# Rotary scores on one core: four of the 64 output stores issued as two transfers of 64 rows

## The chip, the cores and the metric

The kernel runs on one core of a Trainium2 chip. The metric is the device time of one execution in microseconds (us), shown as the median of several runs; one further execution is recorded by the hardware profiler, and all durations of single instructions and transfers come from that one.

## The reference

q and k have the shape (16, 512, 16, 64): 16 batches, 512 positions, 16 heads, 64 values, all float32. Both are rotated by position, and then each query is multiplied with each key of its batch and head:

```
q_rot = [q1*cos - q2*sin, q1*sin + q2*cos]      # q1, q2: the halves of the 64 values
k_rot = [k1*cos - k2*sin, k1*sin + k2*cos]
scores = einsum('bshd,bthd->bsht', q_rot, k_rot)   # (16, 512, 16, 512)
```

The inputs are 67 MB, the output is 268 MB. Nothing is reduced away: every score is written to HBM.

## The kernel before

**Tiling.** A batch is cut into four parts of 128 positions (C = 4); position 4p + c lies on partition p of part c. There are so 64 steps, numbered i = 4 * batch + part. One step makes one output tile `st` of 128 partitions (query positions) by 16 heads by 512 key positions, that is 128 rows of 32 KB, 4 MB in all. The same row of a tile lies in one piece in HBM; rows of neighbouring partitions are 128 KB apart there.

**Work of one step** (loop at line 264 for steps 4 to 63). VectorE rotates the q part of step i + 2 and the k part of step i + 5 (`rope`, lines 149 to 154). TensorE transposes rotated parts by 128x128 blocks (line 170), and VectorE or ScalarE copies the four blocks of a bank to SBUF (line 185). Eight times per step, for two heads each, TensorE multiplies (line 201) and ScalarE copies the 128x1024 result from PSUM into `st` (line 208). After the eighth copy, `store` (line 188) issues the whole tile as one DMA from the queue of SyncE (SP). In steps 0 to 3 the tile goes out in four pieces of 1 MB instead (line 211).

**Buffers.** `st` has three buffers. ScalarE's first copy of step i therefore waits until the store of step i - 3 has landed. The inputs of q and k have two buffers each.

**Order of the DMAs.** SP issues everything in the order of the program: a store per step, and behind the store of each step with i % 4 = 2 the load of a batch of q, behind that with i % 4 = 3 a load of a batch of k (2 MB each, line 122). Each issue uses one of eight completion semaphores in turn, and waits until the transfer that used it eight issues earlier has landed.

**Loads that go around one engine.** Five loads (`RELIEVED`, line 74: q of batch 6, k of 7, q of 11, k of 12, q of 15) are issued in pieces (`load_around`, line 86): rows 0 to 119 from GpSimd (POOL) at line 98, and rows 120 to 127 either from POOL (both k loads) or from SP (the q loads, line 111). Small transfers into `scratch` (line 84) before them set at which of the 16 DMA engines POOL's next transfer begins. The loads of q 11 and k 12 are issued around steps 38 and 39.

Of the kernel before, what the change touches and what calls it, by code (L numbers as in the profile page):

```python
# [10 lines left out]
def kernel(  # L11
# [8 lines left out]
    nc = tc.nc  # L20
# [6 lines left out]
    P = 128  # L27
    C = S // P
# [18 lines left out]
    o_v = out.rearrange("b (p c) h t -> b c p h t", c=C)  # L47
# [137 lines left out]
        copy(out=dst, in_=src)  # L185

    def store(i, st):
        nc.sync.dma_start(o_v[i // C, i % C], st)

    def scores(i, p, st):  # L190

        ps = ps_s_pool.tile([P, 2, S], fp32, tag="ps_s", name="ps")
        b = i // C
        if b == 0:
            c, hp = divmod(p, 2)
            lhs, rhs = qT[i][:, C * hp + c], kT[0][:, 2 * i + hp]
        else:
            lhs, rhs = qT[i][:, p], kT[b][:, p]
        for r in range(2):
            po, rh = ps[:, r, :], rhs[64 * r : 64 * r + 64, :]  # L200
            nc.tensor.matmul(  # L201
                out=po, lhsT=lhs[64 * r : 64 * r + 64, :], rhs=rh, start=True, stop=True
            )
        so, si = st[:, 2 * p : 2 * p + 2, :], ps
        if b > 0:
            so = so.rearrange("s r (t c) -> s r t c", c=C)
            si = si.rearrange("s r (c t) -> s r t c", c=C)
        nc.scalar.copy(out=so, in_=si)  # L208
        if b == 0 and p % 2 == 1:
            c = p // 2  # L210
            nc.sync.dma_start(o_v[0, c, :, G * i : G * (i + 1)], st[:, G * c : G * (c + 1)])
        elif b > 0 and p == HP - 1:
            store(i, st)
# [9 lines left out]
    with tc.manual_schedule():  # L223
# [15 lines left out]
        for i in range(C):  # L239
            st = st_first[i] if i < 2 else stage_pool.tile([P, H, S], fp32, tag="stage", name="st")  # L240
# [6 lines left out]
            for p in range(HP):  # L247
# [7 lines left out]
                if p in (2, 6):  # L255
                    m = len(dve) - (4 if p == 2 else 2) - (2 if i == C - 1 else 0)
# [7 lines left out]
        for i in range(C, NST):  # L264
# [10 lines left out]
            st = stage_pool.tile([P, H, S], fp32, tag="stage", name="st")  # L275
# [45 lines left out]
```

## Time and profile before

| | us |
|---|---|
| time, median of 3 runs (lowest to highest) | 793.13 (792.44 to 794.04) |
| span of the profiled execution, first to last instruction | 790.4 |
| TensorE busy (share of the span) | 684.4 (87%) |
| ScalarE busy | 562.0 (71%) |
| VectorE busy | 544.7 (69%) |
| GpSimd busy | 11.9 (2%) |
| from issue to landing of a 4 MB store, median | 24.7 |

The time of the profiled execution itself is not given apart from its span; the median lies 2.7 us above the span, which is what passes ahead of the first and behind the last instruction. The page gives busy time for each compute engine, the busy share and rate of the 16 DMA engines together, the chain of work that ended last, and groups of instructions with the idle time in front of them and what ended it. A "window" below is a stretch of the span in us from its start.

### The profile page before, as it was taken

Reading aid. Unit: us, or ns where it says so; the run is one execution under the profiler, and the core shown is the slowest. Engines: PE = TensorE matmul, PEld = TensorE weight load, DVE = VectorE, ACT = ScalarE, POOL = GpSimd, SP = SyncE. Lnnn points to the kernel's source line nnn. Section 1 sums busy time; section 2 is a strip of 40 time slices with the busy share of each in tenths; the row PEclk is TensorE's granted clock in tenths of the full one; section 3 lists DMA queues with packets and bytes.
Section 4 is the critical chain, followed back from the end, with each engine's and each line's share of the span. In section 5 each row is a group of like instructions: output and inputs, shape, how many; then the busy total and the mean of one; then the engine's idle time right before and its main releaser. Section 6 shows DMA issues by size and latency. Waiting matters only on the chain.

```text
span 790.4 us, 7750 instructions
## 1 busy us (share of the span) xinstructions
PE 684.4 (87%) x3072; PEld 296.4 (38%) x3072; DVE 544.7 (69%) x516; ACT 562.0 (71%) x647; POOL 11.9 (2%) x24
## 2 busy tenths in 40 slices
PE   4989998988988889798996989889899798799960
PEld 2444443433433334343342433334334343344420
DVE  6999988666766678576785767667678487587400
ACT  3888886865857768486785866777577586588770
POOL 0000000000001000000000001000000000000000
PEclk9999999998999999898998989999899899899995
DMA  9999999999999999999999999999999999999997
GB/s 357 417 425 439 429 430 435 425 435 436 429 429 428 413 432 419 433 423 438 433 427 436 426 432 429 422 432 424 430 432 427 436 429 432 430 432 434 432 429 340
DMA packets 18836, 336.18 MB, mean 425 GB/s; under 512 B 2312, under 2 KB 3592, under 8 KB 4616
## 3 DMA queue, kind: packets, MB, share of 16 engines
q1 hardware_dynamic: 16704, 325.46, 96.4%
q0 software_dynamic: 1808, 10.10, 3.1%
q8 instruction: 24, 0.39, 0.2%
q10 hardware_dynamic: 288, 0.13, 0.1%
q14 instruction: 12, 0.10, 0.0%
HBM read 67.24 MB, written 268.44 MB: 425 GB/s over the span
## 4 chain that ended last, share of the span: by engine, by line
DMA 49%; PE 40%; ACT 5%; DVE 3%; issue 1%; ACTq 0%; SPq 0%; DVEq 0%
DMA out_dram<-st 46%; PE ps L201 30%; PE bank L170 10%; ACT st L208 5%; DMA q_sb<-in_q_dram 2%; DVE part L149 1%; DMA early<-in_k_dram 1%; DVE q_sb L150 0%; DVE k_sb L154 0%; DVE k_sb L150 0%; DVE q_sb L154 0%; DVE early L150 0%; DVE kT_t L185 0%; ACTq L316 0%; DVE early L154 0%
## 5 line engine op out<-in xcount | busy, mean ns | idle before, releaser
L208 ACT COPY st<-ps 128x1024 f32<-128x1024 f32 x512 | 495.7, 1020 | 192.6 <-DMA out_dram<-st 109.8
L201 PE MATMUL ps<-kT_t,qT_t 64*128 64x512 f32 x2048 | 544.0, 649 | 67.0 <-ACT st L208 67.0
L201 PEld LDWEIGHTS ps<-kT_t,qT_t 64*128 64x128 f32 x2048 | 183.6, 196 | 256.2 <-issue 133.3
L185 DVE COPY qT_t<-bank 128x512 f32<-128x512 f32 x118 | 81.6, 691 | 193.9 <-PE bank L170 193.9
L170 PEld LDWEIGHTS bank<-ident,q_sb 128*128 128x128 f32 x480 | 54.2, 149 | 99.0 <-issue 96.4
L170 PEld LDWEIGHTS bank<-ident,k_sb 128*128 128x128 f32 x480 | 50.3, 140 | 96.4 <-DVE k_sb L150 39.5
L170 PE MATMUL bank<-ident,q_sb 128*128 128x128 f32 x480 | 85.1, 304 | 0.9 <-PE ps L201 0.9
L170 PE MATMUL bank<-ident,k_sb 128*128 128x128 f32 x480 | 78.5, 286 | 1.6 <-DVE qT_t L185 1.2
L185 ACT COPY kT_t<-bank 128x512 f32<-128x512 f32 x122 | 72.4, 598 | 6.4 <-PE bank L170 6.4
L154 DVE TENSOR_TENSOR k_sb<-k_sb,part 128x1024 f32<-128x1024 f32 x60 | 73.5, 1225 | 2.1
L150 DVE TENSOR_TENSOR q_sb<-q_sb,cos_t 128x1024 f32<-128x1024 f32 x60 | 73.5, 1225 | 2.1
L150 DVE TENSOR_TENSOR k_sb<-k_sb,cos_t 128x1024 f32<-128x1024 f32 x60 | 73.5, 1225 | 2.0
L149 DVE TENSOR_TENSOR part<-q_sb,ss_t 128x1024 f32<-128x1024 f32 x60 | 73.5, 1225 | 2.0
L149 DVE TENSOR_TENSOR part<-k_sb,ss_t 128x1024 f32<-128x1024 f32 x60 | 73.0, 1216 | 0.9 <-DMA k_sb<-in_k_dram 0.7
L154 DVE TENSOR_TENSOR q_sb<-q_sb,part 128x1024 f32<-128x1024 f32 x60 | 72.9, 1216 | 0.0
L170 PE MATMUL bank<-ident,early 128*128 128x128 f32 x64 | 10.5, 315 | 12.4 <-DVE early L154 10.5
L170 PEld LDWEIGHTS bank<-ident,early 128*128 128x128 f32 x64 | 8.3, 161 | 17.4 <-issue 13.4
L149 DVE TENSOR_TENSOR part<-early,ss_t 128x1024 f32<-128x1024 f32 x8 | 9.8, 1222 | 5.8 <-DMA early<-in_k_dram 5.7
L98 POOL DMA_DIRECT2D q_sb<-in_q_dram x3 | 2.3, 752 | 620.2 <-PE bank L170 446.2
L154 DVE TENSOR_TENSOR early<-early,part 128x512 f32<-128x512 f32 x16 | 10.3, 687 | 0.2
L150 DVE TENSOR_TENSOR early<-early,cos_t 128x1024 f32<-128x1024 f32 x8 | 9.8, 1225 | 0.3
L185 ACT COPY qT_t<-bank 128x512 f32<-128x512 f32 x10 | 5.7, 629 | 3.2 <-PE bank L170 3.2
(12 smaller groups left out, 15.9 us busy)
## 6 DMA issues: line engine op xcount, KB each, us to landing
out_dram<-st SPq DMA_DIRECT2D x60, 4096.0 KB, 24.7
k_sb<-in_k_dram SPq DMA_DIRECT2D x13, 2048.0 KB, 28.3
q_sb<-in_q_dram SPq DMA_DIRECT2D x12, 2048.0 KB, 26.5
out_dram<-st SPq DMA_DIRECT2D x16, 1024.0 KB, 13.8
q_sb<-in_q_dram POOLq DMA_DIRECT2D x3, 1920.0 KB, 27.8
k_sb<-in_k_dram POOLq DMA_DIRECT2D x2, 1920.0 KB, 43.3
early<-in_k_dram SPq DMA_DIRECT2D x1, 1536.0 KB
early<-in_q_dram SPq DMA_DIRECT2D x1, 1536.0 KB
```

Source lines behind the costliest of these rows:

```text
L98: nc.gpsimd.dma_start(dst, src)
L149: nc.vector.tensor_tensor(pv, xs, ss, op=mult)
L150: nc.vector.tensor_tensor(xc, xc, cs, op=mult)
L154: nc.vector.tensor_tensor(y, y, z, op=add)
L170: nc.tensor.transpose(bank[:, x, :], src, ident)
L185: copy(out=dst, in_=src)
L201: nc.tensor.matmul(out=po, lhsT=lhs[64 * r : 64 * r + 64, :], rhs=rh, start=True, stop=True)
L208: nc.scalar.copy(out=so, in_=si)
```

## The change

`store` looks at the step number. In steps 33, 35, 37 and 39 it issues two DMAs of 64 rows (2 MB) each in place of one of 128 rows: in steps 33 and 35 rows 0 to 63 and then rows 64 to 127, in steps 37 and 39 rows 64 to 127 and then rows 0 to 63. Both come from the SP queue, directly behind one another. All other steps are as before, and so are the bytes, their addresses and the compute instructions.

```diff
     def store(i, st):
-        nc.sync.dma_start(o_v[i // C, i % C], st)
+        d = o_v[i // C, i % C]
+        m = P // 2
+        parts = {33: (0, m), 35: (0, m), 37: (m, 0), 39: (m, 0)}
+        if i in parts:
+            for x in parts[i]:
+                nc.sync.dma_start(d[x : x + m], st[x : x + m])
+        else:
+            nc.sync.dma_start(d, st)
```

ScalarE's first copy of steps 36, 38, 40 and 42 then waits for two transfers instead of one.

## The prediction

> **What bounds the kernel now.** I read the page's rates first. All 16 DMA engines are busy from end to end:
>
> ```profile
> DMA  9999999999999999999999999999999999999997
> GB/s 357 417 425 439 429 430 435 425 435 436 429 429 428 413 432 419 433 423 438 433 427 436 426 432 429 422 432 424 430 432 427 436 429 432 430 432 434 432 429 340
> q1 hardware_dynamic: 16704, 325.46, 96.4%
> ```
>
> The digit is the busy share in tenths, the line below it the rate in 40 slices of 19.8 us. Only the first and the last slice fall off. The rate is the same whatever the compute engines do, and queue q1, which carries SP's transfers, holds nearly all of it. The trace's packet records say why: each row of 32 KB is one packet, and 7680 of them (60 stores of 128) have a median of 1.213 us. That is 32768 B / 1.213 us = 27.0 GB/s on an engine, times 16 engines 432 GB/s, which is the plateau. So the engines are not waiting, each is at its own pace, and the time is what the slowest engine has to carry.
>
> The chain of work that ended last agrees, and the windows of the end show the transfers alone:
>
> ```profile
> DMA 49%; PE 40%; ACT 5%; DVE 3%; issue 1%; ACTq 0%; SPq 0%; DVEq 0%
> ...
> DMA out_dram<-st 46%; PE ps L201 30%; PE bank L170 10%; ACT st L208 5%; DMA q_sb<-in_q_dram 2%; DVE part L149 1%; DMA early<-in_k_dram 1%; DVE q_sb L150 0%; DVE k_sb L154 0%; DVE k_sb L150 0%; DVE q_sb L154 0%; DVE early L150 0%; DVE kT_t L185 0%; ACTq L316 0%; DVE early L154 0%
> ```
>
> ```profile
> 770.00:780.00 10.00, 0.00 (x0) 0.00 (x0) 0.00 (x0) 0.00 (x0) 0.00 (x0) 0.50 1.01 436
> ```
>
> The last line's columns are window, length, five engines with counts, TensorE's clock, DMA share, GB/s: nothing computes, 436 GB/s flow. The 40% of TensorE in the chain lie beside transfers that were queued before. Who waits for the transfers stands in the views of waits:
>
> ```profile
> ACT st L208 <- DMA out_dram<-st: 109.8, 42, 5.7
> SPq L188 <- ACT st L208: 659.7, 60, 16.7
> ```
>
> ScalarE waits 109.8 us for buffers that drain; SP has nothing to issue for 659.7 us. A transfer that grows slower lengthens the kernel one to one, an issue more does not.
>
> **The change, part by part.**
>
> Issues. Four issues of SP go and eight come. One lasts 0.33 us, and two back to back stand 0.44 us apart (381.25 to 381.69). Four more cost SP 1.8 us, beside its 659.7 us of waiting. A store takes 24.7 us from issue to landing, since some two others are queued ahead; the second half is in its queue long before an engine comes to it. Cost 0; without that backlog it would be 4 x 0.44 = 1.8 us.
>
> Semaphores. Each issue waits for the transfer eight issues back. With the splits, eight issues reach back four steps instead of five or six. ScalarE could not have filled the tile of step i before the store of step i - 3 landed, so the one of step i - 4 is done. Cost 0. ScalarE's first copy in steps 36, 38, 40 and 42 waits for the later half. That is the last row, as before.
>
> Completion records. Each of the four stores ends 16 more times; these records take 9 ns each on an engine. 4 x 9 ns: nothing.
>
> Bytes. Unchanged. If a half of 64 rows is shared by 16 engines, each has 4 packets of it, and 8 of the store, as before.
>
> Partitions. This is the disputed cost. In all stores before, 16 engines read 128 partitions at a time. Now they read 64 partitions, all of one half, and then all of the other. If the reading of a group of partitions has a width of one engine's rate, two engines share it. The trace has no transfer of 64 rows, so I bound it.
>
> Lower end: 0. Rows 120 to 127 of the relieved loads are 8 rows on as many engines, into 8 neighbouring partitions. For q 15 this came at 696 to 700, and the window did not suffer:
>
> ```profile
> 695.00:701.00 6.00, 6.00 (x32) 2.80 (x32) 5.48 (x5) 5.32 (x8) 0.00 (x0) 1.00 1.01 429
> 701.00:711.00 10.00, 10.00 (x52) 4.41 (x50) 8.53 (x9) 8.68 (x11) 0.00 (x0) 1.00 0.99 426
> ```
>
> Most of its 16 KB packets kept 0.611 us though they overlapped.
>
> Upper end: with sharing at half rate all the way a store's 8 packets take 2 x 8 x 1.213 = 19.4 us in place of 9.7. Four of them add 38.8 us. A row that points that way is the earlier relief, where q 6's and k 7's rows 120 to 127 met in those 8 partitions (and q 11's with k 12's again at 504):
>
> ```profile
> 256.00:262.00 6.00, 4.98 (x24) 2.12 (x24) 5.07 (x5) 3.35 (x4) 0.00 (x0) 1.00 0.99 377
> 262.00:272.00 10.00, 9.78 (x48) 4.34 (x48) 7.24 (x7) 7.85 (x10) 0.00 (x0) 1.00 1.01 429
> 504.00:508.00 4.00, 2.20 (x12) 0.89 (x12) 2.19 (x3) 1.23 (x2) 0.00 (x0) 1.00 1.01 377
> ```
>
> The engines are busy, yet 377 GB/s come out instead of 429: packets of 32 KB took up to 1.85 us there. (1 - 377/429) x 6 us = 0.73 us lost for 256 KB that crowded. At that price the 16 MB of the four stores would lose 64 x 0.73 = 47 us, above the ceiling of 38.8. So the crowded row leans to the upper end; the 128 KB that cost nothing were spread over 4 us and rarely met. Both rows write to SBUF, the stores read from it.
>
> What comes off the ceiling is the lag between engines. They do not work in step: the 16 landings of one store are spread over 4.3 us in step 33 and 5.1 us in step 39, by the trace's landing records. Two engines that share meet only while both are in the same half; a lag d saves each of them d in either half, 2d per store. With 16 engines spread over 4.7 us a pair is on average some 1.6 us apart, and the pair that ends last is a closer one; I take 1.0 us (my estimate). Per store 9.7 - 2.0 = 7.7 us, four times 31 us. I take this value, as the crowded row is the nearer one, with 16 packets of one engine after another and not single ones. The sum on the profiled execution: 790.4 + 31 = 821.4 span, plus the 2.7 us outside the span = **824 us**; the median of the runs shown already holds these 2.7.
>
> The Trainium skill speaks against this change. In "SBUF — State Buffer", section "Can I just issue two DMAs to hit both halves?", it says that one DMA at partition 0 and one at 64 gain only 6% over a single one, and the section on the port swizzle gives 196 GB/s for 64 partitions against 328 for 128 at 1 MiB. By that ratio a store would take 9.7 x 328/196 = 16.2 us, four of them 26 us more, 819 us. The quiet window at 695 differs from a strict reading of it, the crowded ones at 256 and 504 agree, and no run here shows 64 rows yet.
>
> **Rivals.**
>
> 1. Sharing costs only in part. If an engine loses a quarter to a half of the 7.7 us (buffers take up short meetings, as they seem to at 695), four stores add 8 to 16 us: 801 to 809 us. For it: the packets at 695. Against: a half of a store is four packets in a row, 4.85 us, not one.
>
> 2. No width is felt on the reading side: not slower, 793 us (791.6 to 794.7). One mechanism: SBUF gives a group of partitions to two engines at full rate. For it: the window 695 to 701. Against: 256 and 504. It decides if the packets of the split stores stay at 1.213 us. The same time results if each half stays on the eight engines which its rows have now.
>
> 3. Both halves go to the same eight engines. These get 8 packets more per store, 4 x 9.7 = 38.8 us: 832 us. The 8-row loads, with 8 packets, show that a transfer need not use all 16; nothing shows that for 64 rows.
>
> 4. Faster. The engines end apart: step 61's store has its first landing at 764.6 and its last at 770.0. If the splits shifted who lags, without sharing cost, at most half of these 5.4 us could be won, and the meeting at 504 with its (1 - 377/429) x 4 = 0.5 us: 3.2 us, 790 us. Against: each engine keeps its bytes, and nothing takes rows off a late engine.
>
> **How the numbers follow.** Sharing in full, 812 to 832 us: 0.42. In part, 795 to 812: 0.20. The same eight engines: 0.03. No cost, within 0.2% (1.6 us, about what a measurement of this kernel tells from no change): 0.22. Faster by more: 0.13. Slower is 0.42 + 0.20 + 0.03 = 0.65. The forecast is the likeliest case's 824. The range leaves out the faster case and the top of the third rival: 791.5 to 833; the likeliest case alone has 812 to 832.
>
> **What would show it.** In the profile after: DMA share still full but GB/s between 250 and 350 in windows around 430 to 440, 455 to 470, 485 to 500 and later; ScalarE's wait for `out_dram<-st` up by some 25 to 31 us from 109.8; the half stores' time to landing well over 24.7 us. If the GB/s row stays at 422 to 436 there, sharing is wrong and rivals 2 or 4 hold. If the busy share of the DMA engines falls toward a half, it is rival 3. If the time moved but the windows after 550 made it, I have the wrong place.

## The result, and the profile after

The changed kernel takes 849.86 us (median, 845.04 to 862.5) against 793.13: a ratio of 1.0685, 95% interval 1.0641 to 1.0728. That is 54 us more by the ratio, slower as forecast, but far above the forecast 824 and outside the range that ended at 833. Run once more beside the later experiments, its median was 845.51 (841.11 to 853.23) against 793.60, 52 us more.

The first profile caught the longest execution (862.5 us, span 860.7), which the ratio leaves out as slow; the lines here are from a second profiled execution of the same kernel, with 841.11 us and a span of 839.3, 48.9 more than before. It is the fastest of the seven executions of this kernel, so what it shows of the loss lies at the lower end. First the page's rates (busy tenths, then GB/s in 40 slices of 21 us):

```profile
DMA  9999999999999999999999999999999999999995
GB/s 360 418 423 439 432 418 436 437 424 430 437 424 426 428 412 433 427 432 436 427 373 340 346 310 265 266 347 359 415 433 426 435 416 417 432 410 424 428 427 251
q1 hardware_dynamic: 16768, 325.46, 95.1%
```

From slice 21 to 28 (420 to 587 us) the rate falls to 265 to 373, although the engines still count as busy and the queue carries the same bytes. That is the stretch of steps 33 to 39. Before and behind it the rate is as it was, but for the last slice (251, where it was 340). The windows divide it (start, end, length, engines, TensorE's clock, DMA share, GB/s):

```profile
400.00:410.00 10.00, 10.00 (x50) 4.43 (x48) 8.53 (x9) 8.67 (x11) 0.00 (x0) 1.00 1.02 437
...
430.00:440.00 10.00, 2.85 (x9) 0.68 (x6) 1.47 (x2) 2.90 (x4) 0.00 (x0) 0.64 0.99 308
440.00:450.00 10.00, 10.00 (x42) 4.66 (x44) 7.15 (x7) 5.96 (x7) 0.00 (x0) 0.85 0.97 287
...
510.00:520.00 10.00, 10.00 (x38) 4.41 (x40) 6.71 (x6) 7.49 (x9) 1.60 (x3) 0.76 0.81 224
...
570.00:580.00 10.00, 9.98 (x50) 4.21 (x48) 7.36 (x7) 8.51 (x10) 0.00 (x0) 1.00 0.82 353
```

Two things are to be seen. From 430 to 450 the DMA share is 0.97 to 0.99 and the rate is two thirds: busy engines that move less. At 510 and 570 the share itself falls to about 0.8: engines without work. The chain and ScalarE's wait for a tile that drains follow:

```profile
DMA 51%; PE 35%; DVE 5%; ACT 5%; issue 1%; ACTq 0%; SPq 0%; DVEq 0%
```

```profile
ACT st L215 <- DMA out_dram<-st: 149.2, 37, 14.6
```

The chain's DMA part rises from 49 to 51%, the wait from 109.8 to 149.2 us, the longest one from 5.7 to 14.6. A half store takes 36.7 us from issue to landing (median), the whole ones 25.1.

The packet records give the sum. All packets' time, divided by 16 engines, was 788.3 us before and is 825.8 now: 37.5 more for the same bytes. The span less this was 2.1 and is 13.5: 11.4 us more in which an average engine had nothing to do, 6.8 of them in the middle and 4.6 in the last 20 us. 37.5 + 11.4 = 48.9, the whole difference of the spans. The execution of 862.5 us has 44.4 more packet time and 26.0 more without work.

### The profile page after: what moved, and what is told of

Its sections match the earlier page's. It is cut to its first block, busy times and chain, and to the rows that moved or that the text cites. A ratio compares the mean times of both kernels' runs of the same rounds, so it can differ in the third digit from the quotient of the medians.

```text
span 860.7 us, 7758 instructions
## 1 busy us (share of the span) xinstructions
PE 691.4 (80%) x3072; PEld 297.7 (35%) x3072; DVE 544.2 (63%) x516; ACT 561.7 (65%) x647; POOL 11.9 (1%) x24
## 4 chain that ended last, share of the span: by engine, by line
DMA 53%; PE 32%; DVE 7%; ACT 4%; issue 1%; ACTq 0%; SPq 0%; DVEq 0%
DMA out_dram<-st 53%; PE ps L208 24%; PE bank L170 8%; ACT st L215 4%; DVE part L149 2%; DVE early L150 1%; DVE early L154 1%; DVE k_sb L154 1%; DVE k_sb L150 1%; DMA early<-in_k_dram 1%; DVE kT_t L185 0%; DVE q_sb L150 0%; DVE q_sb L154 0%; ACTq L323 0%; DVE qT_t L185 0%
## 5 line engine op out<-in xcount | busy, mean ns | idle before, releaser
L170 PE MATMUL bank<-ident,q_sb 128*128 128x128 f32 x480 | 86.9, 308 | 0.9 <-PE ps L208 0.9
L170 PEld LDWEIGHTS bank<-ident,early 128*128 128x128 f32 x64 | 8.3, 161 | 17.9 <-issue 13.8
(12 smaller groups left out, 15.8 us busy)
```

The costliest lines, as they stand in the source:

```text
L170: nc.tensor.transpose(bank[:, x, :], src, ident)
```

## The experiments

Theory A is the prediction's: the partitions 0 to 63, and 64 to 127, each give room for half of the engines. Its rivals are B (64 rows are slow as such), C (twice as many transfers) and D (beside A, idle engines are a part of the loss).

### The disputed cost alone

All computing is left out; one tile is stored, then another loaded, in ten stages one behind the other:

```
stage(st, stores_whole, 0)               # 128 rows
stage(st, stores_halves, 2, (0, m))      # lower, upper half
stage(st, stores_halves, 4, (32, 32))    # both halves from partitions 32 to 95
stage(st, stores_halves, 6, (0, 0))      # both from 0 to 63
stage(st, stores_columns, 8)             # 128 rows, 8 heads each
...
stage(ld, loads_halves, q_v, 8, (0, m))
stage(ld, loads_halves, k_v, 0, (32, 32))
stage(ld, loads_halves, k_v, 8, (0, 0))
```

> Leaves all computing out: six stages that only store (32 MB each, queued back to back, each stage starting when the one before has landed) and four that only load (16 MB, then three of 8 MB). Stages: whole stores of 128 rows; lower then upper half; both halves from partitions 32 to 95; both from 0 to 63; halves by heads (128 rows of 16 KB); upper then lower half; loads whole; loads into lower then upper half; loads into 32 to 95 twice; loads into 0 to 63 twice. At 27.0 GB/s on each of 16 engines 32 MB take 78 us and 8 MB 19 us. Theory A (the reading of one half of the partitions has room for 8 engines, partitions 32 to 95 for 16): lower then upper, both low, and upper then lower take 140 to 160 us, the middle ones and the halves by heads 78 to 82. Theory B (a transfer of 64 rows is slow as such, or uses 8 engines): the middle ones take 140 to 160 too. Theory C (it is only the greater number of transfers): all split stages are alike. Loads by A for both directions: 39 us, then 39, 19, 39; if writing has more room: 39, 19, 19, 19.

Windows inside these stages (only VectorE, GpSimd, clock, DMA share, GB/s here):

```profile
20.00:88.00 68.00, 0.00 (x0) 0.00 (x0) 1.00 1.00 432
110.00:128.00 18.00, 0.00 (x0) 0.00 (x0) 1.00 0.99 224
210.00:224.00 14.00, 0.00 (x0) 0.00 (x0) 1.00 0.41 164
233.00:311.00 78.00, 0.00 (x0) 0.00 (x0) 1.00 1.00 430
322.00:485.00 163.00, 0.00 (x0) 0.00 (x0) 1.00 0.98 203
495.00:574.00 79.00, 0.00 (x0) 0.00 (x0) 1.00 1.00 425
791.00:826.00 35.00, 0.00 (x0) 0.00 (x0) 1.00 0.97 202
865.00:882.00 17.00, 0.00 (x0) 0.00 (x0) 1.00 1.00 427
924.00:960.00 36.00, 0.00 (x0) 0.00 (x0) 1.00 0.96 197
```

Whole stores run at 432 GB/s, lower and upper half in turn begin at 224, both from 0 to 63 stay at 203, while 64 rows from partitions 32 to 95 have 430 and halves by heads 425. The last three lines are the loads: 202, 427, 197. So 64 rows as such are not slow and the number of transfers costs nothing: B and C fall, and A holds for reading and for writing SBUF. (The stage of whole loads began beside the last stores of the stage before it and is not used.) The packets show the price: a 32 KB row took 1.218 us (median) in the whole and the middle stage, 2.548 us in the stage of partitions 0 to 63, that is 2.1 times.

The third line is the stage of lower and upper half at its end, with a share of 0.41. The 16 landings of one transfer were 0.2 us apart at its first half store and 14.1 us at its sixteenth; the engine in front then needed only 4.8 us per half, as if alone, against 9.4 at the start. Engines that alternate between halves drift apart, which fits unequal shares of the contended half. In the stage that stays on one half they are still within 1.1 us at the end. So A's 140 to 160 us were missed in all three stages: from the first issue to the last landing the two alternating stages took 126 and 127 us, as drifting engines meet less, and the one from 0 to 63 took 165, as a packet there takes 2.1 times and not twice as long. The extra packet time was 4.9 us for two half stores in the stage of lower and upper half, and 10.6 in the stage of 0 to 63: a lag relieves halves that meet only halves.

### The same four stores split by heads

```diff
+        if i in (33, 35, 37, 39):
+            for h in (0, H // 2):
+                nc.sync.dma_start(d[:, h : h + H // 2], st[:, h : h + H // 2])
```

> The same four stores are issued as two of 128 rows, eight heads (16 KB of each row) apiece. As many transfers, issues and semaphores as in the changed kernel. Theory A (shared half of the partitions): no cost, 792 to 795 us. Theory C (two transfers for one, their records, issues and waits): as slow as the changed kernel, some 850.

Measured: 793.58 us, ratio 1.0002 (0.9993 to 1.0012). Two of the windows in which the four stores flow, and the first of them in the kernel before:

```profile
429.00:443.00 14.00, 11.11 (x48) 4.59 (x46) 6.97 (x8) 8.29 (x10) 0.00 (x0) 0.88 1.02 438
455.00:468.00 13.00, 11.66 (x57) 5.08 (x56) 10.37 (x10) 8.03 (x10) 0.00 (x0) 1.00 1.00 428
```

```profile
429.00:443.00 14.00, 11.16 (x48) 4.81 (x46) 7.52 (x8) 8.20 (x10) 0.00 (x0) 0.88 1.00 432
```

Full share, full rate. Four more issues, their completion records, their semaphore turns and ScalarE's double wait cost nothing.

### The same four stores, both halves from partitions 32 to 95

```diff
+        if i in (33, 35, 37, 39):
+            for x in (0, m):
+                nc.sync.dma_start(d[x : x + m], st[32 : 32 + m])
```

> The same four stores as two of 64 rows, but both are read from partitions 32 to 95, so that the rows of these four tiles are not the right ones (partitions 0 to 31 and 96 to 127 are not stored, 32 to 95 twice). Theory A: partitions 32 to 95 reach what the 128 reach, 792 to 796 us. Theory B (64 rows are slow as such): 840 to 860.

Measured: 793.52 us, ratio 1.0000 (0.9991 to 1.0010). With the transfers, rows, bytes and issues of the changed kernel and only other partitions, the whole loss is gone:

```profile
429.00:443.00 14.00, 9.73 (x35) 3.98 (x34) 6.62 (x8) 6.38 (x8) 0.00 (x0) 0.76 1.01 434
481.00:495.00 14.00, 10.43 (x44) 4.15 (x40) 7.93 (x8) 8.79 (x10) 2.14 (x4) 0.88 1.01 428
```

This shows A in place. What remains is its size.

### Only step 33 split

```diff
-        parts = {33: (0, m), 35: (0, m), 37: (m, 0), 39: (m, 0)}
+        parts = {33: (0, m)}
```

> Only step 33 is split, lower half first. Theory A with a fixed price per store: 9.7 us times 16 engines are lost once; if the engines share fairly 800 to 803, if one of two goes first 798 to 803. Theory D (a good part of the 57 us comes from engines drifting apart until the three tiles are used up and engines idle, which a single split does not reach): well under a quarter of 57, about 5 to 10 us, 798 to 803. If each split costs the same with no drift needed: 57/4 = 14, 807.

Measured: 806.60 us (802.98 to 808.78), ratio 1.0158 (1.0124 to 1.0191), 12.8 us more. D's 798 to 803 and the 800 to 803 of a fixed price with fair shares are both missed; the price is near a quarter of the four's. The profiled execution (808.78) has 10.4 us more packet time per engine than before and 6.2 us more without work, most of this in the last 20 us: the page's last slice falls to 250 GB/s, where it was 340.

```profile
430.00:440.00 10.00, 5.25 (x22) 2.01 (x18) 1.87 (x3) 3.84 (x4) 0.00 (x0) 0.71 1.02 279
440.00:450.00 10.00, 9.09 (x40) 3.79 (x40) 8.55 (x8) 4.95 (x7) 0.00 (x0) 0.95 0.99 267
450.00:460.00 10.00, 1.94 (x4) 0.51 (x4) 0.00 (x0) 2.84 (x3) 0.00 (x0) 0.56 0.95 352
460.00:470.00 10.00, 10.00 (x48) 4.88 (x48) 7.82 (x8) 7.80 (x10) 0.00 (x0) 0.93 1.01 418
```

The store alone would flow for 9.7 us, and for 19.4 if every packet took twice as long; the lines are low for 30. The landings point to the reason: step 32's spread over 7.0 us, the second half of step 33 over 15.8, from 441.1 to 456.9. By 447.7 twelve of the 16 engines had landed the second half and gone on to the next whole store, while packets that began at 443 to 450 took up to 5.3 us. So engines that are still in the halves are slow beside others that are already in the next whole store, which reads both halves. Which engines share a path no record shows.

### Four splits far apart, and the bar beside them

```diff
-        parts = {33: (0, m), 35: (0, m), 37: (m, 0), 39: (m, 0)}
+        parts = {9: (0, m), 23: (0, m), 33: (m, 0), 47: (m, 0)}
```

> The changed kernel once more, beside the others: 843 to 862 us as before. All theories expect the same; it gives the bar for the other three.

> Four split stores again, two of them upper half first, but far apart: steps 9 and 23 lower first, 33 and 47 upper first. A single split cost 12.8 us, of which the packets' extra time is 143 us over 16 engines, 9.0 each. Theory A alone (each split has its price, wherever it stands): 4 x 12.8 = 51 us more, 845. Theory A with D (the packets' extra 9.0 to 9.7 is paid per split, and splits close together add idle engines because the late engines keep the three tiles from being filled): 36 to 45 us more, 829 to 839, and no window in which the engines' busy share falls under 0.9.

Measured: 835.69 us (828.82 to 839.10), ratio 1.0518 (1.0464 to 1.0572), 42 more, beside 845.51 for the changed kernel. That lies within the 36 to 45 of A with D; A alone, 845, is missed. In the profile the packets' extra time is 37.3 us per engine, as good as the changed kernel's 37.5, but the time without work in the middle is 5.1 us less, and no stretch of 10 us between 10 and 820 has a share under 0.91. Three stretches in which a split store flows:

```profile
145.00:165.00 20.00, 9.20 (x42) 3.63 (x38) 7.57 (x7) 7.51 (x9) 0.00 (x0) 0.82 0.98 308
...
460.00:480.00 20.00, 15.10 (x55) 6.20 (x56) 8.55 (x8) 11.90 (x14) 0.00 (x0) 0.76 0.98 338
635.00:655.00 20.00, 14.71 (x71) 6.25 (x69) 13.32 (x13) 11.24 (x14) 0.00 (x0) 0.95 0.94 262
```

So the sharing is paid per split wherever it stands. Splits close to one another mostly add idle engines, but not always: of six profiled executions of kernels with steps 33, 35, 37 and 39 split (the changed kernel's two, and four with other orders of the halves, below), five have 6.8 to 25.4 us more without work in the middle than the kernel before, and one, all lower half first, has 1.7, as much as the four far apart. In the changed kernel the landings of one transfer were up to 35 us apart (second half of step 37), over three times a whole store's 9.7 us. How that leaves engines idle stands in its trace. Step 39 fills the tile of step 36, whose store landed last at 508.8, and ScalarE waited 9.6 us for that:

```profile
508.93 2.84 ACT L215 COPY st<-ps 128x1024 f32<-128x1024 f32 x3 [9.60 <-DMA out_dram<-st]
```

The columns are start, length, the copies, and in brackets the wait before them. Step 39's store could be issued only at 520.2, while the first engine had been done with step 38's at 510.5; the window from 510 to 520 has the share of 0.81. So with three tiles the slowest engine holds up the next store, and the others run out of work. That a further tile would remove this was not tried: a fourth tile of 32 KB per partition was not built.

### Half the crowding

```diff
+        if i in (33, 35, 37, 39):
+            for x, y in ((32, 96), (0, 32), (96, 128)):
+                nc.sync.dma_start(d[x:y], st[x:y])
```

> The same four stores in three transfers each: rows 32 to 95, then 0 to 31, then 96 to 127. By theory A the first is free and the other two crowd half as many rows as the changed kernel: half the packets' extra time, 4 x 4.5 to 4.9 = 18 to 20 us, with some drift 812 to 825. By theory C (more transfers) it costs more than the changed kernel, over 850.

Measured: 823.07 us (817.11 to 831.09), ratio 1.0345 (1.0277 to 1.0413). More transfers than in the changed kernel, but only 64 of the 128 rows crowded: the packets' extra time is 16.7 us per engine in the profiled execution, under half of 37.5, and the time without work 9.5 more than before. A's 812 to 825 holds, C's over 850 does not. The price goes by the rows that share, not by the transfers.

### The order of the halves

> Steps 33, 35, 37, 39 as in the changed kernel, all four lower half first. If the order matters (the second pair, turned round, brings back engines that the first pair put behind), it is slower than the changed kernel by over 5 us, 855 and more. If the order does not matter: 843 to 862.

> The four splits all lower half first, again, as the bar for the next two: 824 to 846, as before.

> The four splits, all upper half first. With all four lower first the time was 827, with two and two 846. Theory E (the turn from one order to the other costs: engines that got ahead in the first pair run into those behind in the second): 820 to 832, like all four lower first. Theory F (upper first is the dearer order in itself, because of which engines are ahead by then): over 846.

> The four splits, the first two upper half first and the last two lower first, the changed kernel turned round. Theory E: 840 to 855, as the changed kernel. Theory F: about as the changed kernel too, or under it. If neither order nor turn matters and the difference seen is the place in the run: 827 to 846, overlapping both.

The edits are the pairs in `parts` alone. All lower first: 827.23 us (824.72 to 845.71), and a second time 838.54 (834.96 to 862.32). All upper first: 846.84 (843.6 to 862.15). The changed kernel turned round: 846.50 (836.35 to 865.94). Neither expectation for all lower first (855 and more, or 843 to 862) held. The same kernel twice differs by 11 us, and every one has executions from under 845 to over 845. E's 820 to 832 for all upper first is missed, so the turn can't be the whole cost; F's figure for it, over 846, is met by under 1 us, and whether lower first is really some 10 us cheaper stays open. The executions of one such kernel differ by 12 to 30 us, those of before by 2.9 (792.39 to 795.3 over all that ran beside these).

## Why the prediction was wrong

The direction, the place and the mechanism were right: one half of the partitions shared by all engines, in the stretch 430 to 590, with 224 to 385 GB/s at a DMA share that is mostly full, issues and semaphores at no cost. ScalarE's wait rose by 39 us where 25 to 31 was announced. The size was wrong by two terms. The sum gave a span of 821.4 us, the one shown is 839.3: 17.9 are missing, 11.4 in a term that the sum did not have and 6.5 in one that was too small.

- **"So the engines are not waiting, each is at its own pace, and the time is what the slowest engine has to carry."** This step failed, and it is the larger part of what is missing. It was read from the profile of before and carried into the changed kernel, and so the sum put idle engines at nothing. There were 6.8 us of them in the middle, because the last landing of a store came tens of us behind the first and held up the tile, and 4.6 at the end. Without these 11.4 us the execution shown would have taken 829.7, inside the range. In the execution of 862.5 they are 26.0, and over the six profiled executions 6.0 to 30.3, so that none was at 0. The execution of 849.86 us itself was not profiled; how its loss divides is not known.
- **"What comes off the ceiling is the lag between engines ... a lag d saves each of them d in either half."** This step failed by its size. Of the ceiling of 38.8 us, 37.5 were paid, and not 31. A lag does relieve engines that meet only in halves: the lone alternating stage paid 4.9 us per store, less than the 7.7 assumed. But the step looked at the two halves only. The single split in the kernel paid 10.4, although the landings of the store two steps before were already 5.0 us apart, and what it has and the lone stage has not are whole stores before and behind, in flight beside the halves by the landings. That meeting them makes the difference is argued from the landings, not shown by a run of its own. The term is also unsteady: the six profiled executions have 28.8 to 44.4 us of extra packet time, two of them no more than the 31 taken.
- **The ceiling as the top of the range.** It held only if a shared packet takes just twice as long and if nothing but shared time is lost. By the lone stages a shared 32 KB took 2.548 us against 1.218, which makes 4 x 8 x 1.33 = 42.6 us and not 38.8. In the changed kernel single packets took up to 5.2 us, over four times 1.213; more than two engines on one path, or two with very unequal shares, would do that, and no record shows which engine gets which rows of a half store.
- **The 2.7 us outside the span** are 1.8: the times of the single executions lie 1.8 us above their spans (862.5 and 860.7, 841.11 and 839.3). The rest of the 2.7 was the difference between two executions.

By the runs: 790.4 + 37.5 + 6.8 + 4.6 = 839.3 for the span that was shown, and 841.1 for the time.

Rival 1 (sharing in part, 801 to 809) had 1.9 to 3.9 us of packet time per store; the lone alternating stage paid 4.9, the stage on one half 10.6 and the execution shown 9.4. The quiet window at 695 that spoke for it held 8 packets of 16 KB, spread over 4 us, which is probably too few to meet. Rival 2 is refuted by 203 GB/s for reading alone, rival 3 by the packets: in the lone stage of partitions 0 to 63 the 16 landings of a transfer fall within 1.1 us and the share is 0.98, so all engines take part. Rival 4 is refuted by the ratio. The price from the crowded row (47 us) was too high for the packets' time (37.5), and that it comes nearer to the whole loss of 48.9 than the 31 us taken is luck, as it has nothing for idle engines either.

The Trainium skill's rule in "SBUF — State Buffer" ("Can I just issue two DMAs to hit both halves?") pointed the right way. The same page's section "Door 1: The DMA port swizzle" gives 196 GB/s for 64 partitions at 1 MiB, near the 203 here. The estimate of 26 us from its figures was short: their ratio of 328 to 196 is 1.7, where the lone stages have 432 to 203, 2.1, and the estimate has nothing for engines without work.

## What to carry to other kernels

When a kernel is bound by transfers, ask which partitions each transfer touches before asking how many transfers there are: 64 rows of one half ran at half rate, 64 rows across the middle ran at full rate, and twice as many transfers of 128 rows cost nothing. A contended transfer can cost more than its own extra time, since the engines leave it at different times and the buffer comes free only with the last: put a term for the spread of the landings, and for the number of buffers that it uses up, into the sum. An upper end is only an upper end if it names everything that can be lost.

## What the runs showed of the hardware that was not expected

- Stores that alternate between the halves pull 16 engines apart, from 0.2 to 14.1 us in sixteen transfers (5.2 after seven); stores that stay on one half hardly did (1.1 us), and loads into alternating halves did not either (at most 0.3 us in eight).
- Sixteen engines on one half of the partitions take a little over twice as long per packet: 2.548 us for 32 KB against 1.218, and 1.27 to 1.28 us for a 16 KB load against 0.611.
- Partitions 32 to 95 are as good as all 128 for storing (430 GB/s) and loading (427).
